# Ahead of the first expert of a two-layer hybrid decoder: TensorE's idle products and the first weight splits

## The chip, the cores and the metric

One core of one Trainium2 chip runs the whole kernel. The metric is device time in microseconds (us), from the start of the execution to its end on that core. The engines are TensorE (PE, with its weight loads PEld), VectorE (DVE), ScalarE (ACT), GpSimd (POOL) and SyncE (SP), which issues nearly all DMAs. Each engine takes its instructions in the order in which the kernel emits them.

## The reference, cut to what matters

Two layers over 256 tokens of 1024 channels. Each layer is a mixing block, a feed-forward block and a gated embedding. The feed-forward block of the second layer is a mixture of experts, and the change sits at its entry:

```
def _moe_swiglu(x, router_w, wg, wu, wd):          # x: (1, 256, 1024)
    logits = (xt @ router_w).astype(jnp.float32)
    top_val, top_idx = lax.top_k(logits, TOP_K)     # 2 of 8 experts for each token
    gates = jax.nn.softmax(top_val, axis=-1)
    combine = jnp.einsum('nk,nke->ne', gates, jax.nn.one_hot(top_idx, N_EXPERTS, dtype=jnp.float32))
    for e in range(N_EXPERTS):
        out = out + combine[:, e:e + 1] * _swiglu(xt, wg[e], wu[e], wd[e])

def _swiglu(x, wg, wu, wd):
    return (jax.nn.silu(x @ wg) * (x @ wu)) @ wd    # 1024 -> 3584 -> 1024
```

All numbers are float32.

## The kernel before

**Products.** A float32 product is made of float32r products of halves: each operand is split into a high half (hi, a ScalarE copy that rounds to float32r) and the rest (lo, a VectorE subtraction). `mm3` (L402) multiplies hi by hi, hi by lo and lo by hi.

**Weights.** All weights come in loads of 1 MB (128 partitions x 2048 floats) in the fixed order `seq` (L280). `Feed` (L297) runs them: `pump` (L312) issues a load on SP as soon as a raw buffer is free (5 buffers rawp, and 4 rawb for the experts), `high` (L349) splits off hi on ScalarE, `low` (L367) makes lo on VectorE and frees the raw buffer, `take` (L382) hands a pair to the products and `done` (L394) frees the pair's tiles when TensorE is through. There are three hi tiles and a fourth for the experts, and three lo tiles. The first two loads of the experts come, and are split, in two halves each (L323, `whole`, L334).

**The order of the work** is set when the program is built. Main code emits the products; everything else is a generator (a side stream) that yields the engine of its next step, with names of results that must be there. A planner gives each engine a clock and each instruction a cost (L107 to L127: ScalarE 0.2 + columns / 1400, VectorE 0.1 or 0.13 + columns / 960, TensorE in float32r columns / 2400, and 0.2 from one engine to another). `best` (L205) takes the step with the least (time, penalty, index), where the time is when its engine is free and its inputs are there; steps of the feed have the index -1, side streams 0 and up. `force` (L220) emits it, and `emitted` (L225) forces until the names are ready. The feed offers its steps in `due` (L337):

```
            if self.splitc < min(self.loaded, self.hold) and (self.splitq or self.his):
                t = self.raws[self.splitc][2][1 if self.whole() else self.splitq]
                pen = -3.0 if len(self.hl) + len(self.half) < 3 else 0.5
                r.append((max(act.clk, t, 0.0 if self.splitq else self.his[0][0] + LAT), pen, self.high))
            if self.half and not self.keep and (self.half[0][4] or self.los):
```

The load's time t is set in `pump` (L320, L326) as the time of the buffer's freeing or of the load before, plus 2.65 a load; that a load of an expert must wait for the order of the experts isn't in it.

**Entry to the experts** (`moe`, L1049). `choose(t)` (L1074) makes the router's logits of 128 tokens on TensorE (prl) and the two best experts on VectorE; `ranks` (L1118) counts the tokens of each expert on TensorE (prk) and makes the order of the experts and each token's slot on VectorE. SP reads the order (L1431) and can only then issue the experts' loads. `normed` (L1063) makes rh and rl, the halves of the normed tokens. `gather` (L1176) makes P, a matrix of ones and zeros that picks the tokens of the first two experts, and starts four `part`s (L1191): eight products each (pgx), then gx, four ScalarE copies and four VectorE subtractions. The second normed half of the tokens is needed by the last two parts. `turned` (L1207) transposes P (ppt). Then `gate_up` (L1359) and `down` (L1382) run the experts: six loads to a step of 512 hidden channels (two gate, pmg, two up, pmu, two down, pmy, one step later), seven steps an expert. Experts in places 0, 3 and 6 have 128 slots and three products to a block, the others 64 and two. `combine` (L1093) makes the gate weights when the first silu is there.

**Idle products.** `busy(t)` (L1110) is a product whose result nobody reads: one float32 product of 128 x 512, which has no planned cost. It stands once in each `choose`, behind the logits, and twice in `ranks`, behind the products of each half.

**The hold.** `feed.hold` and `feed.keep` (L1169) keep the splits of the experts' weights back from the start of `moe` on. They are let go at L1437, when the last part of the first gather is emitted (L1436).

Of the kernel before, what the change touches and what calls it, by code (L numbers as in the profile page):

```python
# [11 lines left out]
F32R = mybir.dt.float32r  # L12
I32 = mybir.dt.int32
U32 = mybir.dt.uint32
AF = mybir.ActivationFunctionType
# [49 lines left out]
def tile_trunk(ctx, tc, x, par, con, abias, wif, rw, pt, w1, w2, wgu, wdn, wpg, wpp, wm, out):  # L65
    nc = tc.nc
    PSUM = bass.MemoryType.PSUM
    NRAW, NB, NHL = 5, 4, 3
    cst = ctx.enter_context(tc.tile_pool(name="cst", bufs=1))
# [7 lines left out]
    def tok(t):  # L77
        return slice(128 * t, 128 * t + 128)
# [50 lines left out]
    pe, act = Engine(nc.tensor, pe_cost), Engine(nc.scalar, act_cost)  # L129
# [19 lines left out]
    def bank(shape, name):  # L149

        assert freeb
        t, b = freeb.pop(0)
        if cur[0] is not None:
            cur[0].t = max(cur[0].t, t)
        p = ps.tile([128, 512], F32, name=name, tag=f"b{b}")
        p = p[:, :math.prod(shape[1:])]
        if len(shape) == 3:
            p = p.rearrange("p (a b) -> p a b", a=shape[1])
        held[id(p)] = p, b
        return p  # L160
# [4 lines left out]
    def rel(p):  # L165
        freeb.append((now(), held.pop(id(p))[1]))

    def advance(s):

        before, cur[0] = cur[0], s  # L170
        try:
            y = next(s.gen)
            s.next, s.names = y if isinstance(y, tuple) else (y, ())
            s.bank = s.next is pe or "bank" in s.names
            s.names = [n for n in s.names if n != "bank"]
        except StopIteration:
            s.next = None
        cur[0] = before
        if s.next is None and s in sides:
            sides.remove(s)  # L180

    def side(*gens, pen=0):
        for g in gens:
            s = Stream(g, pen)
            s.t, s.e = main.t, main.e
            sides.append(s)
            advance(s)

    def when(e, *names):
        return e, names  # L190

    def set_ready(*names):
        for n in names:
            ready[n] = now()
# [30 lines left out]
    def emitted(*names):  # L225
        while any(n not in ready for n in names):
            force()
# [19 lines left out]
    h = cst.tile([128, 2, D], F32, name="h")  # L247
# [7 lines left out]
    ident = conT[:, C_ID:C_ID + 128]  # L255
# [6 lines left out]
    ones = cst.tile([128, 128], F32, name="ones")  # L262
    nc.gpsimd.memset(ones, 1.0)
    euler = cst.tile([128, 1], F32, name="euler")
    nc.gpsimd.memset(euler, math.e)
    mhalf = cst.tile([128, 8], F32, name="mhalf")
    nc.gpsimd.memset(mhalf, -0.5)

# [11 lines left out]
    seq = []  # L280
# [119 lines left out]
    feed = Feed()  # L400
# [648 lines left out]
    def moe(L, X, nxt):  # L1049
# [24 lines left out]
        def choose(t):  # L1074

            yield when(pe, (X, t, 0))
            pl = bank([128, NE], "prl")
            for k in range(KT):
                if k == KT // 2:
                    yield when(pe, (X, t, 1), (X, 1, "turned"))  # L1080
                pe.matmul(pl, lhsT=X.hi[:, k, tok(t)], rhs=rwT[:, k], start=k == 0, stop=k == KT - 1)
            busy(t)
            set_ready(("logits", t))
            yield dve
            dve.max(top[:, t], pl)
            dve.max_index(idx[:, t], top[:, t], pl)
            rel(pl)
            dve.tensor_copy(idf[:, t], idx[:, t, 0:2])
            dve.tensor_scalar(oh[:, t, 0], experts, idf[:, t, 0:1], None, op0=ALU.is_equal)
            dve.scalar_tensor_tensor(selm[:, t], experts, idf[:, t, 1:2], oh[:, t, 0], op0=ALU.is_equal, op1=ALU.add)  # L1090
            set_ready(("chosen", t))
# [15 lines left out]
            permuted(cp, comb, t)  # L1107
            set_ready(("comb", t))

        def busy(t):  # L1110

            p = bank([128, 512], "busy")
            c, cur[0] = cur[0], None
            pe.matmul(p, lhsT=ident, rhs=h[:, t, 0:512], start=True, stop=True)
            cur[0] = c
            rel(p)

        def ranks():  # L1118

            pr = bank([128, 3, NE], "prk")  # L1120
            for t in range(2):
                yield when(pe, ("chosen", t), ("logits", 1))
                if t:
                    for t2 in range(2):
                        pe.matmul(pr[:, 2], lhsT=ones, rhs=selm[:, t2], start=t2 == 0, stop=t2 == 1)
                    pe.matmul(pr[:, 1], lhsT=ones, rhs=selm[:, 0], start=True, stop=False)
                pe.matmul(pr[:, t], lhsT=tri, rhs=selm[:, t], start=t == 0, stop=True)
                busy(t)
            yield dve

            dve.scalar_tensor_tensor(key, pr[:, 2], 8.0, experts, op0=ALU.mult, op1=ALU.subtract)
            dve.tensor_tensor(sq, key[:, None, :].to_broadcast([128, NE, NE]),
                              key[:, :, None].to_broadcast([128, NE, NE]), op=ALU.is_gt)
            dve.tensor_reduce(place, sq, axis=AX.X, op=ALU.add)
            dve.tensor_tensor(perm, place[:, None, :].to_broadcast([128, NE, NE]),
                              places[:, :, None].to_broadcast([128, NE, NE]), op=ALU.is_equal)
            dve.tensor_tensor(sq, perm, experts[:, None, :].to_broadcast([128, NE, NE]), op=ALU.mult)
            dve.tensor_reduce(key, sq, axis=AX.X, op=ALU.add)
            dve.tensor_copy(order, key)
            set_ready(("order",))  # L1140
            dve.tensor_tensor(rm, pr[:, 0:2], selm, op=ALU.mult)
            for t in range(2):
                permuted(rp, rm, t)
                set_ready(("ranks", t))
            yield when(dve, ("SL", 0, 0))

            dve.tensor_scalar(slots, place, float(MANY), 64.0, op0=ALU.is_lt, op1=ALU.mult)
            dve.tensor_tensor(key, pr[:, 2], slots, op=ALU.subtract)
            rel(pr)
            dve.tensor_reduce(cnt, key, axis=AX.X, op=ALU.max)  # L1150
            dve.tensor_copy(cni, cnt)
            set_ready(("count",))

        def permuted(to, v, t):

            dve.tensor_tensor(sq, perm, v[:, t, None, :].to_broadcast([128, NE, NE]), op=ALU.mult)
            dve.tensor_reduce(to[:, t], sq, axis=AX.X, op=ALU.add)
# [10 lines left out]
        cp = cst.tile([128, 2, NE], F32, name="cp")  # L1168
        feed.hold, feed.keep = feed.splitc, True  # L1169
        side(choose(0), choose(1), ranks(), pen=-3)  # L1170
        side(normed(0), normed(1), pen=-1)
        side(combine(0), combine(1), pen=-2)
# [3 lines left out]
        def gather(j2):  # L1176

            P = F["P"].tile([128, 2, 2, 128], F32R, name="P", tag="P", bufs=1)
            for t in range(2):
                yield when(dve, ("ranks", t))  # L1180
                for j in range(2):
                    e = 2 * j2 + j
                    dve.tensor_scalar(P[:, t, j], iota if SLOTS[e] == 128 else twice, rp[:, t, e:e + 1], None,
                                      op0=ALU.is_equal)
            for j in range(2):
                e = 2 * j2 + j
                Xe[e] = big.tile([128, KT, 2, SLOTS[e]], F32R, name="gx", tag=("al", "xl")[j])
            side(*[part(j2, P, k2) for k2 in range(KT // 2)], pen=-3)
            side(*[turned(2 * j2 + j, P[:, :, j]) for j in range(2)], pen=1)

        def part(j2, P, k2):  # L1191
            ks = (2 * k2, 2 * k2 + 1)
            yield when(pe, ("normed", 0, k2 // 2), ("normed", 1, k2 // 2))
            p = bank([128, 4, 128], "pgx")
            for i2, k in enumerate(ks):
                for t in range(2):
                    for i, a in enumerate((ah, al)):
                        pe.matmul(p[:, 2 * i2:2 * i2 + 2].rearrange("p a b -> p (a b)"),
                                  lhsT=a[:, t, 128 * k:128 * k + 128],
                                  rhs=P[:, t].rearrange("p a b -> p (a b)"), start=t + i == 0, stop=t + i == 2)  # L1200
            xs = [(Xe[2 * j2 + j][:, k], p[:, 2 * i2 + j, :SLOTS[2 * j2 + j]], g[:, k:k + 1])
                  for j in range(2) for i2, k in enumerate(ks)]
            yield from splits(*[(v[:, 0], v[:, 1], src, gk) for v, src, gk in xs])
            rel(p)
            set_ready(("X", j2, k2))
# [208 lines left out]
        def scatter(e, t, N=None):  # L1414
# [17 lines left out]
            order[0:1], engines=(mybir.EngineType.SP,), min_val=0, max_val=NE - 1,  # L1432
            skip_runtime_bounds_check_because="each is a sum of one of the numbers 0 to 7 and of zeros")[1]
        feed.pump()
        side(gather(0), pen=-3)
        emitted(("X", 0, 3))  # L1436
        feed.hold, feed.keep = len(seq), False  # L1437
# [236 lines left out]
```

## Time and profile before

| | |
|---|---|
| median of 3 runs | 1444.83 us (1444.78 to 1452.07) |
| the profiled execution's own time | 1448.48 us |
| its span, first to last instruction | 1446.7 us |
| TensorE busy | 1385.4 us (96%) |
| VectorE busy | 1218.6 us (84%) |
| ScalarE busy | 1050.7 us (73%) |
| GpSimd busy | 57.0 us (4%) |
| mean granted TensorE clock | 0.983 of full |
| read from HBM | 434.86 MB, 301 GB/s over the span |

Times in the rows are from the span's start. The entry to the experts lies between about 486 and 545 us, the experts reach to about 1400 us. Busy time is the time in which an engine has an instruction running; matmuls overlap, so the start-to-start distance of two tells more than the duration of one. A float32 product shows as two records, and the time in brackets behind a row is the idle time of its engine before it and what ended it. PEclk is the granted clock of TensorE as a share of full speed: 1.0 is 2.4 GHz, 0.5 is 1.2 GHz.

### The profile page before, as it was taken

How to read it: one execution, taken by the hardware profiler on the slowest of the kernel's cores; microseconds unless marked ns; L12 is line 12 of the kernel's file. 1: busy time of each engine (PE TensorE's matmuls, PEld its weight loads, DVE VectorE, ACT ScalarE, POOL GpSimd, SP SyncE). 2: the span in 40 equal slices, each digit the busy share in tenths (PEclk: the TensorE clock that was granted, in tenths of full speed). 3: DMA queues.
4: the chain of work that ended last, by engine and by line, in shares of the span. 5: the costliest groups of instructions: out<-in, count | busy, mean ns of one | idle time of the engine just before them, and what ended most of it. 6: DMA issues, size and time to landing. Idle time of an engine off the chain costs nothing. (4 is left out here: it accounts for less than half of the span.)

```text
span 1446.7 us, 18244 instructions
## 1 busy us (share of the span) xinstructions
PE 1385.4 (96%) x6426; PEld 1112.0 (77%) x6426; DVE 1218.6 (84%) x1294; ACT 1050.7 (73%) x1221; POOL 57.0 (4%) x71
## 2 busy tenths in 40 slices
PE   7999999999999989999979999999999999999998
PEld 6777888888877678887767778887777778887766
DVE  5997645457899498899988999889999999889986
ACT  7766544447776477788977987778988887779884
POOL 0211000000032000000000000000000000000000
PEclk9999999999998899999999999999999999999999
DMA  9243655554440099999998999999999999999980
GB/s 358 88 146 124 205 186 191 185 193 146 164 153 2 16 416 421 421 393 375 422 409 319 422 421 421 384 334 352 419 420 421 422 421 406 378 377 362 420 346 29
DMA packets 62610, 437.17 MB, mean 302 GB/s; under 512 B 7088, under 2 KB 7984, under 8 KB 10672
## 3 DMA queue, kind: packets, MB, share of 16 engines
q1 hardware_dynamic: 62352, 435.42, 76.8%
q8 instruction: 52, 0.85, 0.2%
q0 software_dynamic: 160, 0.52, 0.1%
q14 instruction: 46, 0.38, 0.1%
HBM read 434.86 MB, written 1.05 MB: 301 GB/s over the span
## 5 line engine op out<-in xcount | busy, mean ns | idle before, releaser
L101 DVE TENSOR_TENSOR lo<-rawp,hi 128x2048 fp32r<-128x2048 f32 (+1 forms) x336 | 598.6, 1807 | 113.3 <-ACT hi L101 94.8
L101 ACT ACTIVATE hi<-rawp 128x2048 fp32r<-128x2048 f32 (+1 forms) x336 | 504.8, 1527 | 196.2 <-PE pg L101 34.9
L101 DVE TENSOR_TENSOR lo<-rawb,hi 128x2048 fp32r<-128x2048 f32 (+1 forms) x154 | 343.0, 2248 | 17.2 <-PE pmu L101 4.7
L101 ACT ACTIVATE hi<-rawb 128x2048 fp32r<-128x2048 f32 (+1 forms) x154 | 288.0, 1884 | 60.4 <-PE pmu L101 16.3
L101 PE MATMUL pmg<-hi,gx 128*128 128x512 f32 x616 | 222.1, 399 | 6.7 <-ACTq L1377 5.0
L101 PE MATMUL pmy<-hi,mt 128*128 128x512 f32 x616 | 219.9, 396 | 4.9 <-DVE mt L101 3.7
L101 PE MATMUL pmu<-hi,gx 128*128 128x512 f32 x616 | 223.1, 401 | 0.0
L101 PE MATMUL pmg<-lo,gx 128*128 128x512 f32 x448 | 178.5, 398 | 10.0 <-DVE lo L101 9.9
L101 PE MATMUL pmu<-lo,gx 128*128 128x512 f32 x448 | 179.4, 400 | 8.3 <-DVE lo L101 7.3
L101 PE MATMUL pmy<-lo,mt 128*128 128x512 f32 x448 | 178.3, 398 | 1.2 <-DVE lo L101 1.0
L101 PEld LDWEIGHTS pmg<-hi,gx 128*128 128x128 f32 x616 | 116.5, 189 | 30.7 <-ACTq L1377 5.5
L101 PEld LDWEIGHTS pmy<-hi,mt 128*128 128x128 f32 x616 | 116.2, 189 | 28.9 <-DVE mt L101 4.9
L101 PEld LDWEIGHTS pmu<-hi,gx 128*128 128x128 f32 x616 | 116.6, 189 | 23.8 <-issue 0.7
L101 PEld LDWEIGHTS pmu<-lo,gx 128*128 128x128 f32 x448 | 84.6, 189 | 38.1 <-DVE lo L101 21.4
L101 PEld LDWEIGHTS pmg<-lo,gx 128*128 128x128 f32 x448 | 84.9, 190 | 35.4 <-DVE lo L101 18.5
L101 PEld LDWEIGHTS pmy<-lo,mt 128*128 128x128 f32 x448 | 84.7, 189 | 24.7 <-DVE lo L101 7.5
L101 PEld LDWEIGHTS pht<-conT,msg 128*128 128x128 f32 x560 | 72.1, 192 | 14.2 <-ACT msg L101 9.5
L101 PE MATMUL pht<-conT,msg 128*128 128x64 f32 x560 | 71.7, 272 | 2.8 <-ACT msg L101 2.1
L101 DVE SCALAR_TENSOR_TENSOR z<-zpad,parT,z 128x256 f32<-128x256 f32 x120 | 50.9, 478 | 0.3
L101 PE MATMUL pg<-hi,nh 128*128 128x512 f32 x96 | 37.7, 393 | 0.0
L101 PE MATMUL pg<-hi,nl 128*128 128x512 f32 x96 | 37.4, 390 | 0.0
L101 PE MATMUL pg<-lo,nh 128*128 128x512 f32 x96 | 37.4, 390 | 0.0
(299 smaller groups left out, 1896.2 us busy)
## 6 DMA issues: line engine op xcount, KB each, us to landing
rawp<-in_wm SPq DMA_DIRECT2D x184, 1024.0 KB, 8.8
rawb<-in_wm SPq DMA_DIRECT2D x148, 1024.0 KB, 8.6
rawp<-in_w SPq DMA_DIRECT2D x30, 1024.0 KB, 5.0
rawp<-in_wgu SPq DMA_DIRECT2D x22, 1024.0 KB, 4.9
rawp<-in_wdn SPq DMA_DIRECT2D x11, 1024.0 KB, 4.8
rawp<-in_wpg SPq DMA_DIRECT2D x5, 1024.0 KB, 4.9
rawp<-in_wm SPq DMA_DIRECT2D x8, 512.0 KB, 8.2
rawb<-in_wpg SPq DMA_DIRECT2D x3, 1024.0 KB, 10.5
```

The lines of the kernel that those rows point to most:

```text
L101: return fn(*args, **kw)
```

## The change

A tile `spare` of ones in float32r is made on ScalarE at the kernel's start. `busy` takes a count and makes that many float32r products of 128 x 256 from it; the counts are 12 and 10 behind the logits of the two halves, 4 and 24 behind the rank products. And the hold on the splits is let go one step earlier: behind the issue of the experts' first loads, ahead of the first gather.

```
--- before.py
+++ after.py
@@ -263,6 +263,8 @@
     nc.gpsimd.memset(ones, 1.0)
     euler = cst.tile([128, 1], F32, name="euler")
     nc.gpsimd.memset(euler, math.e)
+    spare = cst.tile([128, 256], F32R, name="spare")
+    nc.scalar.activation(spare, ones[:, 0:1].to_broadcast([128, 256]), AF.Copy)
     mhalf = cst.tile([128, 8], F32, name="mhalf")
     nc.gpsimd.memset(mhalf, -0.5)
 
@@ -1079,7 +1081,7 @@
                 if k == KT // 2:
                     yield when(pe, (X, t, 1), (X, 1, "turned"))
                 pe.matmul(pl, lhsT=X.hi[:, k, tok(t)], rhs=rwT[:, k], start=k == 0, stop=k == KT - 1)
-            busy(t)
+            busy((12, 10)[t])
             set_ready(("logits", t))
             yield dve
             dve.max(top[:, t], pl)
@@ -1107,11 +1109,12 @@
             permuted(cp, comb, t)
             set_ready(("comb", t))
 
-        def busy(t):
+        def busy(n):
 
             p = bank([128, 512], "busy")
             c, cur[0] = cur[0], None
-            pe.matmul(p, lhsT=ident, rhs=h[:, t, 0:512], start=True, stop=True)
+            for _ in range(n):
+                pe.matmul(p[:, 0:256], lhsT=spare[:, 0:128], rhs=spare, start=True, stop=True)
             cur[0] = c
             rel(p)
 
@@ -1125,7 +1128,7 @@
                         pe.matmul(pr[:, 2], lhsT=ones, rhs=selm[:, t2], start=t2 == 0, stop=t2 == 1)
                     pe.matmul(pr[:, 1], lhsT=ones, rhs=selm[:, 0], start=True, stop=False)
                 pe.matmul(pr[:, t], lhsT=tri, rhs=selm[:, t], start=t == 0, stop=True)
-                busy(t)
+                busy((4, 24)[t])
             yield dve
 
             dve.scalar_tensor_tensor(key, pr[:, 2], 8.0, experts, op0=ALU.mult, op1=ALU.subtract)
@@ -1432,6 +1435,7 @@
             order[0:1], engines=(mybir.EngineType.SP,), min_val=0, max_val=NE - 1,
             skip_runtime_bounds_check_because="each is a sum of one of the numbers 0 to 7 and of zeros")[1]
         feed.pump()
+        feed.hold, feed.keep = len(seq), False
         side(gather(0), pen=-3)
         emitted(("X", 0, 3))
         feed.hold, feed.keep = len(seq), False
```

## Rows read from the trace of the kernel before

**Rows 1.** Busy time by stretch: engines in us (instructions), granted clock, DMA share, GB/s.

```profile
540.00:560.00 20.00, 20.00 (x92) 16.55 (x91) 18.25 (x13) 14.41 (x9) 0.00 (x0) 1.00 1.02 422
```

**Rows 2.** Waits between 500 and 1420 us: total us, times, longest.

```profile
ACT hi L101 <- DMA rawp<-in_wm: 1.2, 2, 0.8
```

**Rows 3.** Timeline of TensorE ahead of the expert: start us, us, instructions.

```profile
488.00 2.24 PE L101 MATMUL prl<-rwT,nf 128*128 128x8 f32 x16
490.10 2.06 PE L101 MATMUL busy<-h,conT 128*128 128x512 f32 x2
491.95 3.42 PE L101 MATMUL prl<-rwT,nf 128*128 128x8 f32 x16
...
497.36 2.05 PE L101 MATMUL busy<-h,conT 128*128 128x512 f32 x2
...
500.18 1.11 PE L101 MATMUL busy<-h,conT 128*128 128x512 f32 x2
503.61 0.55 PE L101 MATMUL pgx<-P,rh 128*128 128x256 f32 x1 [2.33 <-issue]
```

**Rows 4.** Stretches in which the granted clock changes (PEclk is the third number from the end).

```profile
489.20:489.60 0.40, 0.40 (x4) 0.40 (x4) 0.00 (x0) 0.40 (x3) 0.00 (x0) 0.62 0.00 0
...
499.20:499.60 0.40, 0.40 (x4) 0.40 (x3) 0.00 (x0) 0.00 (x0) 0.00 (x0) 0.58 0.00 0
...
532.00:540.00 8.00, 7.08 (x26) 5.64 (x27) 8.00 (x6) 4.80 (x4) 0.00 (x0) 0.79 1.02 419
```

**Rows 5.** Timeline of TensorE, the gather's end and the expert's start.

```profile
509.26 0.41 PE L101 MATMUL pgx<-P,rh 128*128 128x256 f32 x1
509.47 0.41 PE L101 MATMUL pgx<-P,rl 128*128 128x256 f32 x1
...
510.21 0.28 PE L101 MATMUL pgx<-P,rh 128*128 128x256 f32 x1
510.32 0.28 PE L101 MATMUL pgx<-P,rl 128*128 128x256 f32 x1
...
512.67 0.49 PE L101 MATMUL pmg<-hi,gx 128*128 128x512 f32 x1 [1.63 <-ACT hi L101]
...
524.99 0.39 PE L101 MATMUL pmg<-hi,gx 128*128 128x512 f32 x1
...
530.43 0.39 PE L101 MATMUL pmu<-hi,gx 128*128 128x512 f32 x1
532.92 0.50 PE L101 MATMUL pmu<-lo,gx 128*128 128x512 f32 x1 [2.10 <-DVE lo L101]
...
540.34 0.39 PE L101 MATMUL pmy<-hi,mt 128*128 128x512 f32 x1
```

**Rows 6.** Timeline of ScalarE around the gather.

```profile
492.69 1.95 ACT L101 ACTIVATE rh<-h,nr 128x512 fp32r<-128x512 f32 x3 [1.66 <-POOL nr L101]
506.15 1.03 ACT L101 ACTIVATE gx<-pgx,parT 128x128 fp32r<-128x128 f32 x4 [11.51 <-PE pgx L101]
...
509.50 2.17 ACT L101 ACTIVATE gx<-pgx,parT 128x128 fp32r<-128x128 f32 x8 [0.67 <-PE pgx L101]
```

**Rows 7.** Timeline of VectorE: the last rl, and the lo behind the combine weights.

```profile
503.81 1.41 DVE L101 SCALAR_TENSOR_TENSOR rl<-h,nr,rh 128x512 fp32r<-128x512 f32 x2
...
530.58 2.28 DVE L101 TENSOR_TENSOR lo<-rawb,hi 128x2048 fp32r<-128x2048 f32 x1
```

**Rows 8.** Line 325 on SP: first half load (502.9 to 503.3 us), then fourth load (505.8 to 506.2).

```profile
L325 SPq DMA_DIRECT2D rawp<-in_wm x1: 347/347/347, 503.1 to 503.1; - x1
...
DMA to landing us min/median/max: 3.9/3.9/3.9
...
L325 SPq DMA_DIRECT2D rawp<-in_wm x1: 333/333/333, 505.9 to 505.9; - x1
...
DMA to landing us min/median/max: 10.9/10.9/10.9
```

**Rows 9.** Groups of instructions from 500 to 560 us: count, busy us, mean ns, idle before.

```profile
L101 ACT ACTIVATE hi<-rawp 128x2048 fp32r<-128x2048 f32 x8 | 15.2, 1920 | 6.4 <-PE pmu L101 3.6 <-PE pmy L101 1.6 <-DMA rawp<-in_wm 1.2
```

More of the change, by code (lines that the diff above doesn't have):

```diff
@@ L265, in tile_trunk @@
     nc.gpsimd.memset(euler, math.e)
+    spare = cst.tile([128, 256], F32R, name="spare")
+    nc.scalar.activation(spare, ones[:, 0:1].to_broadcast([128, 256]), AF.Copy)
     mhalf = cst.tile([128, 8], F32, name="mhalf")
@@ L1081, in choose @@
                 pe.matmul(pl, lhsT=X.hi[:, k, tok(t)], rhs=rwT[:, k], start=k == 0, stop=k == KT - 1)
-            busy(t)
+            busy((12, 10)[t])
             set_ready(("logits", t))
@@ L1108, in combine, with busy @@
             set_ready(("comb", t))
-        def busy(t):
+        def busy(n):
             p = bank([128, 512], "busy")
             c, cur[0] = cur[0], None
-            pe.matmul(p, lhsT=ident, rhs=h[:, t, 0:512], start=True, stop=True)
+            for _ in range(n):
+                pe.matmul(p[:, 0:256], lhsT=spare[:, 0:128], rhs=spare, start=True, stop=True)
             cur[0] = c
@@ L1127, in ranks @@
                 pe.matmul(pr[:, t], lhsT=tri, rhs=selm[:, t], start=t == 0, stop=True)
-                busy(t)
+                busy((4, 24)[t])
             yield dve
@@ L1434, in moe @@
         feed.pump()
+        feed.hold, feed.keep = len(seq), False
         side(gather(0), pen=-3)
```

## The prediction

> **What bounds the kernel now.** I read the busy time in stretches first. From 540 us on TensorE is busy for 20.00 of every 20 us at full clock: the row of 540 to 560 stands for four in a row, up to 620 [rows 1]. So the first expert is bound by TensorE once it runs, although the DMA share is 1.0 there as well. The waits say the same: between 500 and 1420 us ScalarE's splits waited for a load of wm for 1.2 us in all [rows 2], and all of that before 533. What is late at the entry to the first expert is therefore late at its end, and no wait for data behind it takes it up.
>
> Next, TensorE's own instructions ahead of the expert. The reader is to see a chain of router products, four idle products and pauses: prl at 488.0, idle products at 490.10 and 500.18, prl of the second half at 491.95, the gather (pgx) from 503.61 [rows 3]. The granted clock falls inside the slice from 489.2, after a stretch of small products, and is back to full inside the slice from 499.2, behind the idle product of 497.36, which followed another almost without a gap [rows 3, 4]. The gather runs mostly at the lower level (1.2 GHz): its products start 0.21 us apart, and 0.12 us at the end, at 2.4 GHz [rows 5].
>
> Last, the entry itself. The first product of the expert starts at 512.67, after 1.63 us in which TensorE waited for ScalarE's first split. A second stall of 2.10 us ends at 532.92, on a lo of VectorE [rows 5], because VectorE had the combine weights in front of it and began that lo only at 530.58 [rows 7]. Behind it the clock is at half for about 3.4 of 8 us (mean 0.79) [rows 4]. From 540.34, the first down product (load c8), all is dense [rows 5].
>
> **The change, part by part.** I call the 1 MB loads of the first expert c0, c1, ...; c0 and c1 come in halves.
>
> *The tile spare.* One ScalarE copy of 256 columns at the kernel's start, ahead of the first norm, where ScalarE has only x to wait for: nothing. If that cover were gone it is one short instruction.
>
> *The idle products.* Each was one float32 product of 512 columns in two passes: 2.06 us at half clock, 1.11 us at full [rows 3]. They become 12, 10, 4 and 24 products of 256 columns, by the pgx spacing 0.21 us each at half clock and 0.12 at full [rows 5]. At half clock: 2.5, 2.1 and 0.8 us for the first three, 5.0 for the last; at full 1.4, 1.2, 0.5 and 2.9. The first three stand in TensorE's queue ahead of products of the chain that makes the order. Whether the order comes earlier hangs on the clock, which rows of before can't settle. If it falls and comes back where it did: 0.5 us longer at the first, as long at the second, 1.2 shorter at the third; but what is saved at the third comes while the full clock is not yet back, so the rank products take up to 1.7 instead of 1.1 us, and the second products start later. I get an order between 0.8 us later and 0.1 earlier and take 0.3 later. If the clock is back after the first 12 products, prl takes 2.24 instead of 3.42 us [rows 3] and all behind it is shorter: about 2.4 us earlier. Were it never to fall: some 3.7 earlier. The last 24 stand behind the chain: in before TensorE idles 2.33 us there until the gather [rows 3], and after the change, as the next part shows, far longer; they cost nothing.
>
> The Trainium skill, "TensorE: Matmul & The Clock Gate", section "Back-to-back issue gap", has N / 2.4 GHz + 2.5 ns, which is 0.109 us for 256 columns at full clock. The rows show 0.12; by the page the 26 products on the chain would be 0.3 us shorter, if the clock were full.
>
> *The hold.* This decides. Before, no split of the first weights may be put in a queue until the gather's last group is there; now they may as soon as the loads have been issued. The queues are in order, so what counts is where the planner puts the splits, and that can be worked out from its costs. Set ScalarE's planned clock to 0 when the hold goes. It has just placed the third rh. VectorE has placed an rl behind that rh (0.2 + 0.66) and twelve small steps (1.86): it stands at 2.73. The planner's due time of a load is not moved to when the order is known: it counts 2.65 per load from when a slot was free, so in its eyes c0 to c8 landed long ago. All splits are due at ScalarE's clock, until the four hi tiles are gone: c0a at 0, c0b at 0.93, c1a at 1.86, c1b at 2.79, c2 at 3.73, c3 at 5.39. The first gx cannot be due before P, an rl and eight gather products: on VectorE lo c0a has equal due time and penalty with P and goes first as the feed's index is -1, so P ends at 4.83, rl at 5.49, pgx at 6.54, gx is due at 6.74. Even with P first it would be 5.58, behind c3's 5.39. So **all six splits of c0 to c3 stand in ScalarE's queue ahead of the first gx**. The last rh follows gx of groups 0 and 1, and its rl stands on VectorE behind their lo steps; groups 2 and 3 of the gather need that rl, and the expert's products stand behind them on TensorE.
>
> On the chip these splits wait for loads that cannot have landed. c0a is issued at 503.1 and lands 3.9 us later, at 507.0; c3 is issued at 505.9 and lands 10.9 us later, at 516.8 [rows 8]. Before, the first gx ran at 506.15 [rows 6]. Now P waits for lo c0a, and ScalarE's queue for c3: 516.8 + 1.92 for its hi [rows 9] = 518.7; eight gx 2.17 [rows 6] = 520.9; the rh 0.65 (three took 1.95) [rows 6] = 521.5; the rl 0.74 (two took 1.41, overlapped) [rows 7] = 522.3; sixteen pgx at half clock 3.4, as TensorE has idled [rows 5] = 525.7. There the expert's first product starts, 13 us behind 512.67.
>
> What comes back: the six splits are done by then, so TensorE finds no late split for c0 to c2. From 525.7 to c8 it needs eight loads of 2.72 us (two take 524.99 to 530.43 [rows 5]) = 21.8, two groups of transposes 0.8 (the 15.35 us from 524.99 to 540.34 leave 0.7 for one, beside four loads, the stall and the slow clock), the slow clock at the start (0 to 1.7 us lost, the fall of before cost 1.7 [rows 4]; I take 0.85), and the stall on the combine. That one is put one load later in VectorE's queue, where three lo tiles lie ready: 0 to its old 2.1 us, I take 0.5, as the lead is then some five us. Sum: 549.6 against 540.34, so +9.3 us; with the order 0.3 later **+9.6 us**. SP's issues keep their order; c9 and c10 wait for the lo of c0 and c1 on VectorE, as before, and eleven loads queued keep the DMA going until after 530.
>
> A rule on the loads: the Trainium skill, "DMA: Bandwidth & Descriptors", section "Anatomy of one DMA", fits 2.0 us plus bytes / 436 GB/s, given there for GpSimd's path. By it four loads land by 514.7 (an estimate) and the whole is 2.1 us less, 1452.3 us. The row says 516.8, so the trace differs.
>
> The profiled execution took 1448.48 us, its span 1446.7; the median of three is 1444.83, 3.65 below. The difference is put on the median: 1444.83 + 9.6 = 1454.4 us.
>
> **The rivals.**
> *The idle products lift the clock early (0.20).* Dense short products bring the full clock back before the second prl: order and all loads 2.4 us earlier instead of 0.3 later, the rest as above: +6.9, 1451.7 us. For it: two idle products in a row had it back at 499.2 [rows 3, 4]. Against it: the one of 2.06 us at 490.10 alone did not, and the gather's products, from 503.61 on, were at the lower spacing still at 509.26 [rows 3, 5]. The Trainium skill, same TensorE page, section "What's actually happening", has it that activity releases the throttle; by that rule alone this case would be the forecast.
> *VectorE gives P the first turn (0.10).* If lo c0a does not go ahead of P, the last rh is due when c2 is placed and wins against c3 by its penalty. On the chip it then runs by 516.8 at the latest, its rl by 518.2, the last gather products by 521.6: the expert starts 4.1 us before 525.7, +5.5, 1450.3 us. Against it: the tie and the index in the code.
> *Faster: the splits fall into ScalarE's gaps (0.12).* If gx is placed ahead of c1 or c2, ScalarE has c0a at 507.0 and uses the gaps in the gather. The expert starts when the transposes end, near 511.0, with lo ready: 3.1 us ahead of the effective start of before (524.99 less four loads = 514.1); if with it the combine falls behind a lo that isn't needed yet, the 2.1 us stall and the 1.7 us of slow clock go too: -6.9, 1437.9 us. It decides where the first gx starts: by 507 it is this case, after 518 the forecast. Against it speaks the planner's sum above.
>
> **How the numbers follow.** The forecast has 0.58, the rivals 0.20, 0.10 and 0.12. 0.5% is 7.2 us, about what a measurement of this kernel can tell from no change. The forecast's own range, with clock loss 0 to 1.7, stall 0 to 2.1 and order 0.8 late to 0.1 early, is 1452.7 to 1457.4. To hold the clock rival and the first-turn case the range is 1447 to 1458; the faster case is left out. Over 7.2 us slower: nearly all of the forecast (0.53) and a part of the clock rival (0.07), 0.60. Within: the rest of these (0.18), the first-turn case (0.10) and a third of the faster one (0.04), 0.32. Faster by more, which takes the faster case together with an earlier order: 0.08.
>
> **What would show it.** In the profile after: hi of c0 to c3 ahead of the first gx on ScalarE, each ended by a DMA wait; the first gx near 518.7; TensorE idle or in idle products from about 503 to 510 and again to 522; the first pmg near 525.7 and the first pmy near 550; behind it the same dense stretches. A first gx before 510 makes the forecast wrong; a first load issued before 502 speaks for the clock rival; a pmg near 522 for the first-turn case.

## The result, and the profile after

| | before | after |
|---|---|---|
| median | 1448.20 us, 8 runs (1440.66 to 1452.07) | 1456.21 us, 8 runs (1453.24 to 1459.14) |
| ratio, 95% interval | | 1.0065 [1.0045, 1.0085] |
| the profiled execution | 1448.48 us, span 1446.7 | 1453.24 us, span 1451.5 |
| a second profiled execution (last runs below) | 1444.73 us, span 1443.0 | 1455.91 us, span 1454.1 |

The change is slower by 0.65% by the ratio, 9.4 us on 1448 (the two medians differ by 8.0). The two profiles first shown differ by 4.8 us only. Both numbers are needed: the profiled execution of before was one in which the clock fell in the router chain, and the second one, in which it did not, is 3.75 us faster.

**TensorE**, its timeline in the profile after (start, duration, instructions, in brackets the idle time before and what ended it):

```profile
488.21 1.85 PE L101 MATMUL prl<-rwT,nf 128*128 128x8 f32 x16
489.92 1.68 PE L101 MATMUL busy<-spare 128*128 128x256 f32 x12
491.43 1.85 PE L101 MATMUL prl<-rwT,nf 128*128 128x8 f32 x16
493.14 1.44 PE L101 MATMUL busy<-spare 128*128 128x256 f32 x10
...
495.92 3.10 PE L101 MATMUL busy<-spare 128*128 128x256 f32 x24
...
505.62 0.55 PE L101 MATMUL pgx<-P,rh 128*128 128x256 f32 x1 [6.59 <-ACT hi L101]
...
516.55 0.58 PE L101 MATMUL pgx<-P,rh 128*128 128x256 f32 x1 [6.46 <-ACT rh L101]
520.56 0.63 PE L101 MATMUL pmg<-hi,gx 128*128 128x512 f32 x1
...
545.09 0.39 PE L101 MATMUL pmy<-hi,mt 128*128 128x512 f32 x1
```

Beside [rows 3] the second prl takes 1.85 instead of 3.42 us and the rank products are through at 496. Then come two holes of 6.6 and 6.5 us, on both sides of the gather's first half, that before did not have. The first pmg starts at 520.56 instead of 512.67, the first pmy at 545.09 instead of 540.34 [rows 5].

**ScalarE**, its timeline after, tells what the holes wait for:

```profile
492.51 1.34 ACT L101 ACTIVATE rh<-h,nr 128x512 fp32r<-128x512 f32 x2 [1.25 <-POOL nr L101]
502.81 1.06 ACT L101 ACTIVATE hi<-rawp 128x1024 fp32r<-128x1024 f32 x1 [8.96 <-DMA rawp<-in_wm]
...
509.65 1.91 ACT L101 ACTIVATE hi<-rawp 128x2048 fp32r<-128x2048 f32 x1 [1.48 <-DMA rawp<-in_wm]
512.13 1.91 ACT L101 ACTIVATE hi<-rawp 128x2048 fp32r<-128x2048 f32 x1 [0.57 <-DMA rawp<-in_wm]
513.94 1.95 ACT L101 ACTIVATE gx<-pgx,parT 128x128 fp32r<-128x128 f32 x8
515.73 0.77 ACT L101 ACTIVATE rh<-h,nr 128x512 fp32r<-128x512 f32 x1
```

Six splits stand between the second rh and the first gx, each behind a load; where [rows 6] had ScalarE waiting for pgx, it now waits for DMA. The pgx of the first two groups were done by 510, their gx came at 513.94, and the rh that the other two groups need at 515.73. **VectorE** shows the same turn, P behind the first lo:

```profile
503.90 1.23 DVE L101 TENSOR_TENSOR lo<-rawp,hi 128x1024 fp32r<-128x1024 f32 x1 [5.04 <-ACT hi L101]
505.04 0.87 DVE L101 TENSOR_SCALAR P<-conT,rp 128x128 fp32r<-128x128 f32 x4
```

The stretches after, to be read beside [rows 4] and [rows 1] (engines in us, granted clock third from the end):

```profile
489.20:489.60 0.40, 0.40 (x6) 0.40 (x5) 0.00 (x0) 0.40 (x3) 0.00 (x0) 1.00 0.00 0
499.20:499.60 0.40, 0.00 (x0) 0.00 (x0) 0.00 (x0) 0.00 (x0) 0.00 (x0) 1.00 0.00 0
532.00:540.00 8.00, 7.91 (x37) 6.37 (x36) 7.21 (x20) 5.65 (x4) 2.39 (x2) 1.00 0.84 346
540.00:560.00 20.00, 20.00 (x91) 16.55 (x91) 19.93 (x12) 15.03 (x12) 0.00 (x0) 1.00 0.96 360
```

The clock stays at full through the router chain, and the fall between 532 and 540 (0.79) is gone with the stall ahead of it. From 540 on TensorE is as dense as before, so what is late there stays late.

The first load on SP (line 327 now, 498.6 to 499.2 us), beside [rows 8]:

```profile
L327 SPq DMA_DIRECT2D rawp<-in_wm x1: 348/348/348, 498.8 to 498.8; - x1
...
DMA to landing us min/median/max: 4.0/4.0/4.0
```

**One scale for all runs.** The stages ahead of the router are the same in all kernels, but they end up to 3.7 us earlier or later from one execution to the next (first prl at 488.0 to 491.7). So the table gives us behind the first prl of the same profile. For the kernel after: 498.8 less 488.2 is 10.6, 513.94 less 488.2 is 25.7.

| kernel | first load issued | first gx | first pmg | first pmy | end of the span | ratio to before |
|---|---|---|---|---|---|---|
| before | 15.1 | 18.1 | 24.7 | 52.3 | 958.7 | |
| before, second profile | 10.0 | 12.6 | 18.9 | 45.5 | 953.3 | |
| after | 10.6 | 25.7 | 32.4 | 56.9 | 963.3 | 1.0065 |
| after, second profile | 10.6 | 25.7 | 32.3 | 56.5 | 965.1 | |
| idle products alone | 10.6 | 13.1 | 17.9 | 47.3 | 956.8 | 0.9979 |
| hold alone | 13.3 | 29.1 | 35.7 | 59.8 | 968.8 | 1.0065 |
| hold, c0 alone | 14.9 | 24.1 | 27.7 | 54.1 | 962.7 | 1.0025 |
| hold, ScalarE's half alone | 10.0 | 23.8 | 28.4 | 56.4 | 966.0 | 1.0099 |
| experts in own order, before | -46.7 | 12.6 | 18.9 | 45.4 | 953.1 | 0.9990 |
| experts in own order, hold | -48.1 | 17.7 | 25.1 | 49.4 | 958.1 | 0.9999 |
| after, all due times moved | 10.6 | 13.1 | 16.1 | 45.9 | 957.9 | 1.0010 |
| after, four due times moved | 10.6 | 13.1 | 16.1 | 49.2 | 958.7 | 0.9998 |
| idles alone, combine late | 10.6 | 13.1 | 18.0 | 42.7 | 957.7 | 1.0010 |
| idles alone, no last 24 | 10.6 | 13.7 | 20.3 | 46.8 | 954.0 | 0.9986 |

### The profile page after: what moved, and what is told of

The parts are those of the page before. It is cut to its first block, busy times and chain, and to the rows that moved or that the text cites. A ratio compares the mean times of both kernels' runs of the same rounds, so it can differ in the third digit from the quotient of the medians.

```text
span 1451.5 us, 18322 instructions
## 1 busy us (share of the span) xinstructions
PE 1380.7 (95%) x6468; PEld 1110.5 (77%) x6468; DVE 1218.4 (84%) x1294; ACT 1052.4 (73%) x1222; POOL 57.1 (4%) x71
## 5 line engine op out<-in xcount | busy, mean ns | idle before, releaser
L101 PEld LDWEIGHTS pmg<-hi,gx 128*128 128x128 f32 x616 | 117.0, 190 | 28.4 <-ACTq L1380 4.9
L101 PEld LDWEIGHTS pmu<-lo,gx 128*128 128x128 f32 x448 | 84.2, 188 | 35.9 <-DVE lo L101 18.9
```

The source lines that it names most:

```text
L101: return fn(*args, **kw)
```

## The experiments

My theory: the hold costs what the forecast says, because splits of loads that have not landed stand in in-order queues ahead of the gather; the idle products give little. The first rival: the idle products are the cost, or both. The second: what costs is the splits' own time ahead of gx, not the wait for loads.

### Which half of the change costs: the halves alone

The idle products alone, out of the kernel after:

```
         feed.pump()
-        feed.hold, feed.keep = len(seq), False
         side(gather(0), pen=-3)
```

> The changed kernel with the hold let go where it was before: only the idle products are new. Theory (the loss is the early splits in ScalarE's queue; the idle products cost nothing and, where the clock stays up, bring the order forward): 0 to 4.3 us faster than before, ratio 0.997 to 1.000; first gx 4.1 us behind the first load's issue as before, expert's first product some 9.6 us behind that issue. Rival 1 (the idle products are the loss, since TensorE is held up or its clock lost): the 8 us of the whole change appear here, ratio 1.0055 or more. Rival 2 (splitting while the gather runs costs by itself): as the theory.

Measured: 0.9979 [0.9959, 0.9998], 1445.98 us in 12 runs. The first pmg comes 7.3 us behind the first issue, earlier than the 9.6 expected; the run without the last 24 idle products, below, tells why.

The hold alone, on the kernel before:

```
         feed.pump()
+        feed.hold, feed.keep = len(seq), False
         side(gather(0), pen=-3)
```

> The kernel before with the hold let go early and nothing else: float32 idle products stay. Theory: six splits stand ahead of the first gx on ScalarE; first gx 15 us behind the first load's issue (503 to 518.7), expert's first product near 525.7, first pmy near 549.6; +9.3 us, ratio 1.0064 (1.005 to 1.008). Rival 1: no slower than before, ratio 0.998 to 1.002. Rival 2: as the theory.

Measured: 1.0065 [1.0039, 1.0091], 1459.18 us in 8 runs. ScalarE's timeline has the queue of the kernel after, later by the later order:

```profile
508.79 1.06 ACT L101 ACTIVATE hi<-rawp 128x1024 fp32r<-128x1024 f32 x1 [11.78 <-DMA rawp<-in_wm]
...
518.65 1.91 ACT L101 ACTIVATE hi<-rawp 128x2048 fp32r<-128x2048 f32 x1 [0.89 <-DMA rawp<-in_wm]
520.47 1.94 ACT L101 ACTIVATE gx<-pgx,parT 128x128 fp32r<-128x128 f32 x8
```

The hold is the cost, the idle products a small gain of 0.2%. The two halves add to 1.0044, just below the interval of the whole; with the intervals that the halves have themselves this is no contradiction.

### How much of the hold: fewer splits, and ScalarE's alone

Only c0 let go early, on the kernel before:

```
         feed.pump()
+        feed.hold, feed.keep = feed.splitc + 1, False
         side(gather(0), pen=-3)
```

> The kernel before, the hold let go early for the first load alone (two half splits instead of six splits). Theory (the price is the wait for the last load split ahead of gx): ScalarE is held for c0b only, which lands 6.4 us behind the order instead of 14.8, and VectorE's P waits for lo of c0a, so the gather's products start 6 to 7 us later than before and the first gx near 512 to 513; the lo of c1 to c4 follow some 5 us late: +5 us, ratio 1.0035 (1.002 to 1.005), about half of e2. Rival 2 (splits among the gather cost by their own time): two halves of 1.07 us, +2 us at most, ratio 1.0015 or less.

Measured: 1.0025 [1.0001, 1.0049]. ScalarE now has only the two halves of c0, and the third rh, ahead of gx, and is through with them at 511.4. What the first gx then waits for is the gather itself: P, at 510.49, stands on VectorE behind lo c0a, which waits for the split of the first half that has landed:

```profile
508.26 1.06 ACT L101 ACTIVATE hi<-rawp 128x1024 fp32r<-128x1024 f32 x1 [13.12 <-DMA rawp<-in_wm]
...
509.35 1.23 DVE L101 TENSOR_TENSOR lo<-rawp,hi 128x1024 fp32r<-128x1024 f32 x1 [4.93 <-ACT hi L101]
...
513.61 1.04 ACT L101 ACTIVATE gx<-pgx,parT 128x128 fp32r<-128x128 f32 x4 [2.23 <-PE pgx L101]
```

The first gx is 9.2 us behind the issue, against 3.0 in the first profile of before and 15.1 in the kernel after. So fewer loads queued ahead cost less, and with c0 alone the delay comes by VectorE's queue.

All of ScalarE's splits early, VectorE's kept back:

```
         feed.pump()
+        feed.hold = len(seq)
         side(gather(0), pen=-3)
```

> The kernel before; the hold on ScalarE's hi splits is let go early, that on VectorE's lo (keep) stays until the gather is out. So P no longer stands behind lo c0a, only gx behind six hi. Theory (ScalarE's queue holds gx until c3 has landed): the gather's first products run within 1 us of where they ran before (0.5 us behind the first load's issue), yet the first gx comes only 15 to 16 us behind that issue (before: 3.0), and the lo of c0 and c1 come after the gather's last subtraction, so the expert starts some 10 us late: +6 to +10 us, ratio 1.004 to 1.007. Rival (the price is VectorE's queue, P behind lo c0a): no more than 2 us slower, ratio 1.0015 or less.

Measured: 1.0099 [1.0072, 1.0127], only 4 runs; the direction as expected, more than expected, and not below the hold alone. P is early here and so is the first half of the gather, and it helps nothing:

```profile
500.49 0.55 PE L101 MATMUL pgx<-P,rh 128*128 128x256 f32 x1 [2.33 <-issue]
...
513.82 0.58 PE L101 MATMUL pgx<-P,rh 128*128 128x256 f32 x1 [8.76 <-ACT rh L101]
...
521.04 0.80 PE L101 MATMUL pmg<-lo,gx 128*128 128x512 f32 x1 [2.01 <-DVE lo L101]
```

The gather's second half waits for the rh on ScalarE, and the kept lo steps bring a stall of 2.01 us of their own. ScalarE's queue alone is enough for the cost. What VectorE's turn ahead of P adds to it, this run does not tell apart: the first pmg is 18.4 us behind the issue against 21.8 in the kernel after, but with the lo steps kept back the first pmy is at 46.4 against 46.3.

### The wait for loads, or the splits themselves

In these two the loads don't wait for the order: the experts run in their own numbering, so the loads land long before the gather (the first is issued some 47 us ahead of the first prl). The order of the experts is made but not used, so another result is computed, with the same amount of work.

```
+        feed.order = list(range(NE))
+        feed.pump()
...
-        feed.order = nc.values_load_multi_w_load_instructions(
+        nc.values_load_multi_w_load_instructions(
```

> Control for the next run. The kernel before, but the experts' loads don't wait for the order: they are issued from the start of the block, experts in their own numbering (so each block of slots is multiplied by another expert's weights; same shapes, same amount of work). The hold is where it was. All of c0 to c8 have landed before the gather. Theory: the first split still stands behind the last gx, so the first product comes where it did, 24.7 us behind the first router product: ratio 0.998 to 1.001.

> As the control, loads early and experts in their own numbering, and the hold let go early as in the change: the same six splits ahead of the first gx, but their loads have landed. Theory (the price is the wait for loads that haven't landed, not the splits): six hi take 4 x 1.07 + 2 x 1.92 = 8.1 us in the 11.5 us in which ScalarE idled; first gx within 2 us of before (18.1 us behind the first router product), expert's first product 26 to 28 us behind it (before 24.7, with hold only 35.7), first pmy at most 1 us behind before's 52.3: ratio 0.998 to 1.0015. Rival 2 (splits among the gather cost by themselves, by order and by time): still 4 to 9 us slower, ratio 1.003 to 1.0065.

Measured: 0.9990 [0.9970, 1.0010] without the hold's line and 0.9999 [0.9977, 1.0021] with it. With the loads there, the six splits run back to back in a gap of ScalarE:

```profile
497.18 7.48 ACT L101 ACTIVATE hi<-rawp 128x1024 fp32r<-128x1024 f32 x6
509.33 1.03 ACT L101 ACTIVATE gx<-pgx,parT 128x128 fp32r<-128x128 f32 x4 [4.67 <-PE pgx L101]
```

ScalarE then waits for pgx, not the other way round. The same line that costs 0.65% costs nothing that can be measured when the loads have landed; the second rival falls. (The two profiles differ by 5.0 us at the end. In the one with the hold the clock fell in the router chain, in the other it did not; the medians of ten runs do not show that difference. Counted from VectorE's first step behind the rank products, key, at 495.83 without the hold's line and 502.40 with it, the first pmy comes 38.0 and 38.6 us later, so the line costs 0.6 us there.) Loads 57 us earlier than in the second profile of before gave nothing either: the first pmg is at 18.9 in both.

### The planner's due times put right

The kernel after, with the planner told that the loads wait for the order:

```
+        feed.dma = max(feed.dma, ready["order",] + 1.8)
         feed.pump()
```

> The changed kernel, and the planner's DMA clock is set to its time of the order plus 1.8 before the experts' first loads are issued, so that the due times of the loads agree with the chip (c0a due some 5 us behind the order, 2.65 a load). The hold is let go early as in the change. Theory: the planner now puts the splits into ScalarE's and VectorE's gaps of the gather, c1b and later behind the last gx; the first gx is again 4 us behind the first issue, the expert's first product at most 8 us behind it (before: 9.6), and the stall on the combine shrinks: 3 to 9 us faster than before, ratio 0.994 to 0.998. Rival 2: still slower than before by 4 us or more, as splits run among the gather's. Rival 1: still slower by some 8 us, since the idle products are the same.

Measured: 1.0010 [0.9993, 1.0027]. The queue is mended, the first pmg is, with 16.1, earlier than in all runs so far, and the ratio missed its expectation. As that line also moves the times of all later loads, a second form moves the first four alone:

```
         feed.pump()
+        for n in range(4):
+            raw, which, t = feed.raws[first_moe + n]
+            at = ready["order",] + 3.8 + 2.65 * (n + 1)
+            feed.raws[first_moe + n] = raw, which, [at - 1.3 * (1 - q) * (n < 2) for q in range(2)]
         feed.hold, feed.keep = len(seq), False
```

> The kernel after, with the planner's due times of the first four loads alone set behind the issue of the first load (3.8 us plus 2.65 us a load, halves 1.3 earlier), the clock of the planner's later loads untouched. Theory (the price of the change is only that the splits stand ahead of P and gx while the loads have not landed; with true due times the queues put them behind): first gx 13.1 us and first pmg 16 to 18 us behind the first prl, as in the earlier run with moved due times, and, since later loads keep their places, less of it is given back: ratio 0.995 to 0.998. Rival (what is gained at the entry is given back in the later experts, whatever the places): ratio 0.998 to 1.002, with the first pmy 5 us or more early and the last product within 2 us of the kernel before.

Measured: 0.9998 [0.9982, 1.0013]. ScalarE takes the splits in its gaps between the gx, as the forecast's faster rival had it:

```profile
502.93 1.97 ACT L101 ACTIVATE gx<-pgx,parT 128x128 fp32r<-128x128 f32 x8 [6.84 <-PE pgx L101]
504.74 2.05 ACT L101 ACTIVATE hi<-rawp 128x1024 fp32r<-128x1024 f32 x2
506.69 1.02 ACT L101 ACTIVATE gx<-pgx,parT 128x128 fp32r<-128x128 f32 x4
```

The hold's line is at the same place as in the kernel after, and its whole cost is gone: so the cost is the queue's order, and that came from the due times. But both forms gain nothing on the kernel before, against my expectation; the ratio lies in the rival's range. Where that start goes is in TensorE's stalls between the first pmg and the first pmy of the second form:

```profile
505.90 0.50 PE L101 MATMUL pmg<-hi,gx 128*128 128x512 f32 x1 [0.20 <-ACT hi L101]
507.16 0.50 PE L101 MATMUL pmg<-lo,gx 128*128 128x512 f32 x1 [0.76 <-DVE lo L101]
510.33 0.50 PE L101 MATMUL pmg<-lo,gx 128*128 128x512 f32 x1 [0.16 <-DVE lo L101]
515.52 0.50 PE L101 MATMUL pmu<-lo,gx 128*128 128x512 f32 x1 [1.53 <-DVE lo L101]
529.43 0.61 PE L101 MATMUL pmu<-lo,gx 128*128 128x512 f32 x1 [2.60 <-DVE lo L101]
537.40 0.66 PE L101 MATMUL pht<-conT,msl 128*128 128x128 f32 x4 [0.41 <-DVE msl L101]
539.04 0.50 PE L101 MATMUL pmy<-hi,mt 128*128 128x512 f32 x1 [0.98 <-ACT mt L101]
```

The stalls behind the first pmg add to 6.4 us, four of the six on a lo. ScalarE's splits meanwhile wait for DMA and begin 2.5 us apart (four from 511.23 to 518.75): TensorE has run into the loads and what is made of them. (The planner also orders TensorE's products otherwise here, so its first pmy is not quite the same milestone.)

### What an earlier start is worth: the combine, and the last 24 idle products

The idle products alone, and the combine put one load later on VectorE:

```
-            yield when(dve, ("SL", 0, 0), (X, t, "r"))
+            yield when(dve, ("SL", 0, 1), (X, t, "r"))
```

> The idle products alone (hold as before), and the combine weights wait for the second silu instead of the first, so that no lo of the first two hidden steps stands behind them on VectorE. Theory (the stall of 2.1 to 2.6 us on the lo behind the combine and the half clock behind it are worth 3.8 us and a gain at the entry is kept): first pmy 43 to 44.5 us behind the first router product (idle products alone: 47.3); 3 to 4 us faster than the idle products alone, ratio to before 0.994 to 0.997. Rival (entry gains are given back at the branch on the count in the third expert, where the idle products alone lost 3 of their 5 us): ratio 0.9975 to 0.999.

Measured: 1.0010 [0.9992, 1.0028], a miss, above the rival's range too, which was nearer. The stall has moved, from a pmu to a pmy, and is as long. First the idle products alone, then this run, both TensorE:

```profile
530.57 0.50 PE L101 MATMUL pmu<-lo,gx 128*128 128x512 f32 x1 [2.63 <-DVE lo L101]
```

```profile
538.93 0.80 PE L101 MATMUL pmy<-lo,mt 128*128 128x512 f32 x1 [2.57 <-DVE lo L101]
```

Its first pmy stands ahead of that stall, 4.6 us earlier than without the edit; at the second gather's first gx the two are equal again (240.4 and 240.6 behind the first prl). Then the last 24 idle products taken out:

```
-                busy((4, 24)[t])
+                if not t:
+                    busy(4)
```

> The kernel with the idle products alone (hold as before), with the last 24 idle products, those behind the rank products of the second half, taken out (12, 10 and 4 stay). Theory (the 24 keep the clock at full through the pause ahead of the gather, and that is why the gather ran at 0.12 us spacing there): the gather's products start 0.21 us apart, the first pmg comes 20 to 21 us behind the first prl instead of 17.9, and the ratio to before is 0.998 to 1.001, 1 to 3 us above the 0.9979 of the idle products alone. Rival (the 24 do nothing: the clock would have stayed full anyway, since the rank products and the pause are short): gather at 0.12 us, pmg at 17.9, ratio as with them.

Measured: 0.9986 [0.9971, 1.0002]. The first reading is as the theory has it. TensorE with the 24:

```profile
498.39 3.10 PE L101 MATMUL busy<-spare 128*128 128x256 f32 x24
501.83 0.36 PE L101 MATMUL pgx<-P,rh 128*128 128x256 f32 x1 [0.34 <-issue]
...
503.06 0.28 PE L101 MATMUL pgx<-P,rh 128*128 128x256 f32 x1
503.18 0.28 PE L101 MATMUL pgx<-P,rl 128*128 128x256 f32 x1
```

and without:

```profile
502.32 0.55 PE L101 MATMUL pgx<-P,rh 128*128 128x256 f32 x1 [3.40 <-issue]
...
504.02 0.41 PE L101 MATMUL pgx<-P,rh 128*128 128x256 f32 x1
504.23 0.41 PE L101 MATMUL pgx<-P,rl 128*128 128x256 f32 x1
```

Spacing 0.12 and 0.21 us, so the 24 do hold the clock over a pause in which the chain is on VectorE, and the first pmg is 2.3 us earlier with them. At the first pmy nothing of it is left (47.3 with, 46.8 without): the stalls ahead of it are 4.4 us with them (0.76, 1.00 and 2.63) and 0.75 without, where the expert's start runs at half clock to about 518.5 instead. The two intervals overlap in most of their length; the runs do not tell whether the 24 are worth anything.

### Does the clock fall in every execution?

Both kernels once more, for a second profile.

> The kernel before, a second profile. Theory (with the float32 idle products the clock in the router chain differs from run to run): the first load is issued anywhere from 10 to 15.1 us behind the first prl, and not at the 15.1 us of the first profile alone; a value within 0.3 of 15.1 would speak for a fixed fall of the clock in this kernel.

> The kernel after, a second profile. Theory (the float32r idle products keep the clock at full through the router chain in every execution): the first load is issued 10.4 to 10.8 us behind the first prl, as in four profiles so far. Rival (it differs from run to run as with the float32 ones): anywhere from 10 to 15 us.

Measured: 1444.73 us for before, its first load issued 10.0 us behind the first prl; 1455.91 for after, 10.6 again. TensorE in the second profile of before, beside [rows 3]:

```profile
489.68 1.85 PE L101 MATMUL prl<-rwT,nf 128*128 128x8 f32 x16
491.39 1.10 PE L101 MATMUL busy<-h,conT 128*128 128x512 f32 x2
492.33 1.85 PE L101 MATMUL prl<-rwT,nf 128*128 128x8 f32 x16
```

The same instructions with no fall: prl 1.85 instead of 2.24 and 3.42 us, idle products 1.10 instead of 2.06. Of seven profiles with the float32 idle products four have the fall (first issue at 13.3 to 15.1 us, or in the one whose loads don't wait for the order the second prl at 2.52 us), three have none; of seven with the float32r ones none has it (10.6 in each).

## Why the prediction was right, and where it was not

**The hold: right, by its mechanism and its size.** The six splits stand ahead of the first gx, each ended by a load, P behind lo c0a, the last rh behind eight gx. The text had the first load's issue at 503.1, 0.3 us late left out:

| behind the first issue, us | forecast | after |
|---|---|---|
| first gx | 518.7: 15.6 | 513.94 less 498.8: 15.1 |
| first pmg | 525.7: 22.6 | 21.8 |
| first pmy | 549.6: 46.5 | 46.3 |

The stall on the combine, taken as 0.5 us, is none; the slow clock at the expert's start is there, up to about 523.5, which makes some 1.4 us where the text took 0.85. In before the first pmy stood 37.2 us behind the issue (52.3 less 15.1) in the profile that the forecast used, 35.5 in the second one; after has 46.3 and 45.9. By the difference, from 45.9 less 37.2 to 46.3 less 35.5, the hold takes 8.7 to 10.8 us at the first pmy, forecast 9.3. The hold alone has the same distance, 46.5. The dense stretches keep what is late: +4.6 us on the first profile of before at the first pmy, +4.6 at the end. That loads not landed are its cause is shown by the runs with the loads landed (0.9999) and with due times put right (0.9998, 1.0010): the same line, no cost.

**The order: the term that failed.** The text took the order 0.3 us later, "if it falls and comes back where it did". Against the profile that it used the order is 4.5 us earlier (10.6 instead of 15.1 behind the first prl): the clock never falls. That is the clock rival's mechanism, at more than its 2.4 us and near the 3.7 that the text gave for a clock that never falls. The sum for this pair of profiles is then +9.3 less 4.5, +4.8 us, and they differ by 4.8.

**Why the forecast time was still near.** The forecast was +9.6 us, the runs have +9.4 by the ratio (+8.0 by the medians shown first). The rows that price the idle products came from an execution with the fall, but a good part of the executions of before must have none (three of seven profiles with the float32 idle products). Against such a one the order is 0.6 later (10.6 against 10.0), and after is 10.0 to 11.8 us later at the end (963.3 and 965.1 against 953.3); against one with the fall it is 4.6 to 6.4. The measured ratio lies between. So the median came near 1454.4 (measured 1456.21) with the order's term right only against one kind of execution and 4.5 us off against the other. That the whole came so near is in part luck, the more as the median of three that it was added to, 1444.83, is 3.4 us below the median of eight.

**The other parts.** The last 24 idle products cost nothing, as said; in the kernel after they also bring nothing, as 6.59 us of idling follow and the gather runs at 0.21 us spacing all the same. The mark for the first-turn case, "a pmg near 522", was badly chosen: 520.56 is nearer to it than to 525.7. It was an absolute time, and the order moved; from the issue, that case has 521.6 less 503.1, 18.5 us, the measured 21.8, and P stands behind lo c0a. Such marks should be given as distances. The faster rival, splits in ScalarE's gaps, came true in the run with four due times moved, with the first pmg at 16.1, 8.6 us ahead of the first profile of before and 2.8 ahead of the second. But it gave 0.9998 and not the -6.9 us of the text: that sum took the stall on the combine for gone, where 2.60 us stayed, and an early start for kept, where 6.4 us of stalls, these 2.60 among them, took most of it back.

**The two rules weighed.** The fourth load's split began 13.3 us behind the first issue (512.13 less 498.8); the row had 13.7. The Trainium skill's fit in "DMA: Bandwidth & Descriptors", section "Anatomy of one DMA", made that 11.6 (an estimate), so the row was the one to take on SP's path. The clock in the router chain stayed at full in all seven profiles with dense idle products. The rule that activity releases the throttle, in the Trainium skill's "TensorE: Matmul & The Clock Gate", section "What's actually happening", agrees with that. Why the same sparse products have the fall in four profiles and not in three, no run here shows.

**A version that beats both kernels** is the idle products alone, 0.9979 [0.9959, 0.9998]. It is a small gain, the interval ends just below 1, and what it can consist of by the rows is the router chain without its fall: 10.6 in every profile instead of 10.0 to 15.1. No run shows that this is all of it.

**Left open.** The idle products alone are 5.0 us ahead of the first profile of before at the first pmy and 1.9 at the end; most of that goes between the second gather and the third (first gx 240.6 against 245.8 behind the first prl, then 477.3 against 479.2). The granted clock shows where. One row each for before, the idle products alone, after, and after's second profile, from some 13 us ahead of the second gather's first gx on (engines in us, granted clock third from the end):

```profile
721.00:790.00 69.00, 59.13 (x278) 47.37 (x277) 59.51 (x54) 51.84 (x59) 0.00 (x0) 0.95 0.91 366
718.00:787.00 69.00, 58.13 (x262) 46.35 (x261) 56.33 (x53) 48.59 (x55) 0.00 (x0) 0.90 0.90 347
726.00:795.00 69.00, 59.70 (x286) 48.01 (x285) 60.35 (x55) 52.60 (x60) 0.00 (x0) 0.95 0.94 367
726.00:795.00 69.00, 60.21 (x272) 48.11 (x272) 58.67 (x54) 50.76 (x58) 0.00 (x0) 0.90 0.92 358
```

A mean of 0.95 over 69 us is some 7 us at half clock, 0.90 some 14; the 7 more are worth about 3.4 us (an estimate from these rows). From the second gather's first gx to the third's it takes 233.4, 236.7, 232.3 and 234.4 us in these four. So the idle products alone lose their 3.3 us where the clock was down longer, and the two profiles of the kernel after, 0.4 apart at the first pmy, come to differ by 1.8 at the end in the same place. As the kernel after shows both, this differs between executions of one kernel and need not be a price of the idle products. Why the clock is down longer in some is not shown. Why the hold with ScalarE's half alone costs 1.0099, above the whole hold's 1.0065, is not settled; the intervals overlap.

## What to carry to other kernels

A step that waits for a transfer blocks all that stands behind it in its engine's queue: before letting such steps go early, check that the planner's time for the transfer includes what the transfer itself waits for, here the order of the experts. An earlier start is worth nothing where the next thing in line is already late; look for the stall that takes its place before you count it. And where a clock or a stage differs from one execution to the next, take the price of a term from several profiles, since one profile shows only one of the cases.

## What the runs showed of the hardware that was not expected

The clock in one and the same stretch of one and the same kernel falls in some executions and not in others: 1.2 GHz from 489.2 us on in the first profile of before, 2.4 GHz to past 498 in the second, which makes 5 us at the order. A second such place lies behind the second gather: of the fourteen profiles five have some 7 us at half clock there, two some 10 and seven some 14, and both kernels' kinds of idle products are among the five and the seven. The mean granted clock goes with the time in the runs of one kernel: among 23 runs of before timed with the last experiments, 1442.87 us had 0.989 and 1452.89 us 0.978, with a correlation of -0.94 over all 23. With the idle products of 256 columns in float32r, 12 and 10 in a row, none of seven profiles had that fall.
